# Eleven scan slots in place of fourteen for every 64 projection steps

## The chip, the cores and the metric

The kernel runs on one NeuronCore of a Trainium2 chip. TensorE (PE) multiplies matrices and writes to PSUM; PEld is its loading of the stationary operand; VectorE (DVE), ScalarE (ACT) and GpSimd (POOL) do the elementwise work; SyncE (SP) issues the DMAs. The metric is the device time of one execution in microseconds, the median of several runs.

## The reference

A trunk of two layers works on 256 tokens of width 2048. Each layer normalizes x, projects it to one wide row, passes that to two groups of heads and projects their joined output back onto x:

```python
for l in range(DEPTH):
    h = rms_norm(x, norm_g[l])
    proj = jnp.einsum('btd,dc->btc', h, w_in[l])
    rw_in, g_rw, q, k_at, v_at, g_at = jnp.split(proj, col_splits, axis=-1)
    ...
    y_rw = rwkv7_branch(r, k, v, xw, xa, ...)
    ...
    y_at = window_attention(qh, kh, vh, sink[l]).astype(x.dtype)
    mix = jnp.concatenate([y_rw * jax.nn.silu(g_rw), y_at * jax.nn.silu(g_at)], axis=-1)
    x = x + jnp.einsum('btc,cd->btd', mix, w_out[l])
return rms_norm(x, final_g)
```

The first group has 16 heads of 64 with a recurrent state, once forwards and once backwards in time:

```python
def step(S, inp):
    r_t, w_t, k_t, v_t, kk_t, a_t = inp
    s_kk = jnp.einsum('bhvk,bhk->bhv', S, kk_t)
    S = (S * w_t[:, :, None, :]
         - s_kk[..., None] * (a_t * kk_t)[:, :, None, :]
         + v_t[..., None] * k_t[:, :, None, :])
    return S, jnp.einsum('bhvk,bhk->bhv', S, r_t)
```

The sum of both directions is normalized per head; a bonus term times v is added. The second group is attention in a band of 128 tokens with a sink logit per head.

## The kernel before

**Projections.** The activations lie transposed, 16 tiles of 128 channels by 256 tokens. The kernel wants more than one rounded product gives, so every operand is split into a high part and a remainder (XH, XL and MH, ML for the activations; hi, lo for the weights), and one step is three products of 128x128 by 256 columns (L292 to L294, in `gemm`). An output tile of 128 columns takes 16 steps. `wsplit` makes the weights' parts, hi on ScalarE (L222) and lo on VectorE (L224), one half tile (8 steps) at a time, with two buffers. `Stream.run(n)` emits the next n steps; `Stream.later(n, f)` calls f after n steps.

**Scan.** The recurrence is computed in four chunks of 64 tokens (NC) for a pair of heads at a time; NP = 8 pairs in a layer, with both directions in one tile. It has three generators, and every `yield` in them is a place where the projections may go on:
- `scan_p(p)` prepares: low-rank products (pza, L671 to L673), decays (VectorE's scans), head sums (pk), scaled keys (BK, MV), the bonus (pbn). 13 parts.
- `scan_i(p)` forms the Gram rows GE of the chunks (pg, L786, masked by L792), transposes (pt: L809 the centred values, L817 the keys), and inverts a unit triangular matrix over six levels. The levels swap between products of TC into QF (L899, with a turn L866) and products of QF back into TC (L908, taken in by VectorE's L910); at the end come pf, then pn and its copy VF. 16 parts.
- `scan_b(p)` carries the state SUV through the four chunks: L957, copied to RH; L964, L970, L973, copied into SUV by L975; L980, taken by VectorE into the next chunk's state (L982); and the output products L987 into py. Then the norm of py: squares with row sums (L998), a power on GpSimd (L1000), the multiply by it, the products L1007, and the last steps into MH and ML. 17 parts.

**The order of work.** TensorE's order is the program's order, written out by hand: `manual_schedule` covers PE. For the other engines a planner orders the instructions by its own costs and by priority; `high_priority` lifts single ones, and what is called through PA or PV keeps the program's order among itself. Each engine then runs its list in order. `window(64, ...)` (L394) spreads the parts of several generators over SLOTS = 14 slots; after each slot's parts it runs 64/14 (4 or 5) projection steps. `scans(w)` says which pairs are in which phase in window w: preparation of pair w-1 (its tail, pair w-2), `scan_i` of pair w-2 in all slots and its last two parts at the start of the next window, `scan_b` of pair w-3 from slot 1 on, and its last four parts one window on. The order of the list of stages is the order of emission within a slot. Window 12 has attention alone; windows 10 and 11 have it beside the scan's end. After window 12 the output projection runs by itself (256 steps). ROT spreads the set-up of the rotary tables over layer 0's windows.

**Memory.** Tiles of a tag with `bufs=n` rotate over n buffers; a write waits until the readers of the tile n takings ago are done. `big` has four operand tiles of 16 by 256 floats a partition: X0, then XH, XL, MH, ML of the layers in turn. In PSUM, `ps_main` holds two projection tiles, `ps_w` two pairs of banks that all of `scan_p`, `scan_i` and the attention take in turn (`wpair`, `wbank`), and `ps_c` one bank for the state (pcc) and one for the output sums (py).

Of the kernel before, what the change touches and what calls it, by code (L numbers as in the profile page):

```python
# [21 lines left out]
T = 256  # L22
# [33 lines left out]
ROT = {0: [2, 3], 1: [], 7: [3, 6, 9], 8: [1, 4], 9: []}  # L56
# [78 lines left out]
def hybrid_trunk_kernel(ctx, tc, xT, wi, wv, wo, par, fing, dup, iup, sink, pos, cst, out):  # L135
# [11 lines left out]
    big = pool("big", 4)  # L147
# [31 lines left out]
    def bigt(dt, name):  # L179
        return big.tile([128, NKT, T], dt, tag="big", name=name)  # L180
# [123 lines left out]
    X0 = bigt(F32, "X0")  # L304
# [13 lines left out]
    AB, AL, QF = (cp.tile([128, 2, NC, 64], F16, name=n) for n in ("AB", "AL", "QF"))  # L318
# [289 lines left out]
    def queue_output(l):  # L608
# [4 lines left out]
        def tile_of(k):  # L613
# [6 lines left out]
            def evac(pm):  # L620
                if last and k == 0:
                    L.X2 = bigt(F32, "X2")
# [3 lines left out]
                if k == 0:  # L626
                    to.norm = Norm()
                    to.acc = st("acc", [T])
                    if not last:
                        to.XH, to.XL = bigt(F32R, "XH"), bigt(F32R, "XL")  # L630
# [24 lines left out]
    def layer(l):  # L655
# [3 lines left out]
        L.MH, L.ML = MH, ML = bigt(F32R, "MH"), bigt(F32R, "ML")  # L659
# [30 lines left out]
        def scan_p(p, t):  # L690
# [9 lines left out]
            LW = st("lw", [2 * T])  # L700
# [32 lines left out]
            BK = st("bk", [2, NC, 3, 64])  # L733
            km = st("lw", [2 * T])
# [14 lines left out]
            PA.activation(BK8[64:128, :, 0, :], BK8[64:128, :, 2, :], AF.Copy)  # L749
            yield  # L750
# [13 lines left out]
            bonus = high(km[:, 0:T], "th")  # L764
# [11 lines left out]
        def scan_i(p, t):  # L776
            VV, BK, MV = t["v"], t["BK"], t["MV"]
            flat = lambda x: x.rearrange("p d c j -> p (d c) j")
            GE = st("ge", [2, 2, NC, 2, 64], bufs=2)
# [26 lines left out]
            for b in range(2):  # L806
                for q in range(2):
                    for h in range(2):
                        PE.matmul(  # L809
                            pts[h][half[q], 384 + b * 64 : 448 + b * 64], VV[half[h], cs(2 * b + q)], cen[half[h], half[h]], start=True, stop=True  # L810
                        )

# [10 lines left out]
            SUV = st("suv", [2, NC, 2, 64], bufs=2)  # L823
            t["SUV"] = SUV
            for h in range(2):
                for q in range(2):
                    A.activation(
# [418 lines left out]
```

## Time and profile before

| what | us |
|---|---|
| median of 3 runs (lowest, highest) | 1187.84 (1186.2, 1188.79) |
| span of the profiled execution | 1186.6 |
| PE, DVE, ACT busy in it | 1160.9, 908.2, 777.3 |
| a scan window in steady state (one pair in each phase) | 41.2 |
| output projection of the last layer, to its last product | 90.5 |

The profile gives single times of one execution, the median is over others. Rows that begin with a time are instructions in order of time: start, duration, engine, line, operation, result and operands, tile shape on the array, size, count in a row, and in brackets idle time and what ended it. Matmuls overlap, so a row's duration is not its cost; the distance from start to start is. Rows that begin with a line number are groups of like instructions: total busy time, mean ns of one, and idle time before them by what ended it.

### The profile page before, as it was taken

What the parts mean: (1) busy time and instruction counts of PE and PEld (TensorE: products, weight loads), DVE (VectorE), ACT (ScalarE), POOL (GpSimd) and SP (SyncE); (2) the same over time, 40 slices, a digit from 0 to 9 for tenths busy, and PEclk for the clock granted to TensorE, in tenths of its full rate; (3) what the DMA queues carried; (4) which work ended last, traced back from release to release, by engine and by line L of the source; (5) the groups of instructions that cost most, each with busy time, mean ns of one, the idle gap of its engine ahead of it and who ended that gap; (6) DMA issues with size and microseconds to landing.
All of it is one profiled execution on the core that took longest, in us unless ns stands there. A gap on an engine that the chain in (4) does not pass through costs nothing.

```text
span 1186.6 us, 38095 instructions
## 1 busy us (share of the span) xinstructions
PE 1160.9 (98%) x16151; PEld 1082.7 (91%) x16151; DVE 908.2 (77%) x2017; ACT 777.3 (66%) x1955; POOL 18.7 (2%) x23
## 2 busy tenths in 40 slices
PE   8999999999999999999999999999999999999996
PEld 6988998999889989899999999999999998889996
DVE  6889878987877678766677988887887866786654
ACT  6666776777776666645555766876777666665553
POOL 0000000000000000000000000000000000000000
PEclk9999999999999999999999999999999999999998
DMA  7553333333323434477664443333323334345653
GB/s 257 164 170 123 109 107 116 108 98 115 109 94 122 136 117 142 134 234 236 210 184 165 134 131 114 95 113 117 122 83 109 122 124 132 114 145 190 213 185 123
DMA packets 60410, 166.63 MB, mean 140 GB/s; under 512 B 7728, under 2 KB 22736, under 8 KB 60240
## 3 DMA queue, kind: packets, MB, share of 16 engines
q1 hardware_dynamic: 60240, 164.21, 43.0%
q8 instruction: 126, 2.06, 0.7%
q14 instruction: 44, 0.36, 0.1%
HBM read 157.37 MB, written 4.19 MB: 136 GB/s over the span
## 4 chain that ended last, share of the span: by engine, by line
PE 74%; issue 15%; DVE 7%; ACT 2%; POOL 1%; DMA 1%; SPq 0%; DVEq 0%; POOLq 0%; ACTq 0%
PE pm L292 19%; PE pm L294 16%; PE pm L293 16%; PE pg L786 3%; DVE lo L224 2%; PE pcc L957 2%; PE py L987 2%; PE py L964 1%; PE pcc L980 1%; PE pq L899 1%; PE pcc L970 1%; PE pd L908 1%; PE pza L671 1%; POOL yv L1000 1%; PE pscr L1050 1%
## 5 line engine op out<-in xcount | busy, mean ns | idle before, releaser
L292 PE MATMUL pm<-XH,hi 128*128 128x256 f32 x1664 | 494.2, 297 | 3.9 <-ACT XH L184 1.6
L294 PE MATMUL pm<-XH,lo 128*128 128x256 f32 x1664 | 467.8, 281 | 5.9 <-DVE lo L224 5.8
L293 PE MATMUL pm<-XL,hi 128*128 128x256 f32 x1664 | 467.6, 281 | 0.8 <-DVE XL L185 0.6
L222 ACT ACTIVATE hi<-raw 128x512 fp32r<-128x512 f32 x560 | 328.2, 625 | 190.6 <-PE pm L293 91.8
L224 DVE TENSOR_TENSOR lo<-raw,hi 128x512 fp32r<-128x512 f32 x560 | 369.1, 686 | 102.5 <-ACT hi L222 95.2
L292 PEld LDWEIGHTS pm<-XH,hi 128*128 128x128 f32 x1664 | 313.4, 188 | 19.3 <-ACT XH L184 2.6
L294 PEld LDWEIGHTS pm<-XH,lo 128*128 128x128 f32 x1664 | 313.9, 189 | 8.3 <-DVE lo L224 8.3
L293 PEld LDWEIGHTS pm<-XL,hi 128*128 128x128 f32 x1664 | 314.1, 189 | 1.7 <-DVE XL L185 1.7
L292 PE MATMUL pm<-MH,hi 128*128 128x256 f32 x512 | 144.0, 281 | 0.0
L294 PE MATMUL pm<-MH,lo 128*128 128x256 f32 x512 | 143.8, 281 | 0.0
L293 PE MATMUL pm<-ML,hi 128*128 128x256 f32 x512 | 143.8, 281 | 0.0
L292 PEld LDWEIGHTS pm<-MH,hi 128*128 128x128 f32 x512 | 96.6, 189 | 0.8 <-issue 0.8
L293 PEld LDWEIGHTS pm<-ML,hi 128*128 128x128 f32 x512 | 96.6, 189 | 0.0
L294 PEld LDWEIGHTS pm<-MH,lo 128*128 128x128 f32 x512 | 96.6, 189 | 0.0
L910 DVE CAST_PREDICATED tv<-LV,pd 128x256 f16<-128x256 uint8 x80 | 34.2, 428 | 12.0 <-PE pd L908 11.4
L1065 ACT ACTIVATE mv<-mv,mx 128x257 f32<-128x257 f32 x64 | 31.9, 503 | 17.2 <-DVE mx L1062 17.2
L792 DVE TENSOR_TENSOR ge<-pg,C 128x1024 f32<-128x1024 f32 x32 | 38.8, 1219 | 2.3 <-PE pg L786 2.3
L975 ACT ACTIVATE suv<-pcc 64x128 f32<-64x128 f32 x128 | 34.3, 268 | 9.2 <-PE pcc L973 7.4
L959 ACT ACTIVATE rh<-pcc 128x128 f32<-128x128 f32 x64 | 17.5, 274 | 34.0 <-PE pcc L957 33.6
L902 ACT ACTIVATE QF<-pq 128x256 f16<-128x256 f32 x80 | 30.8, 384 | 12.5 <-PE pq L866 11.7
L786 PE MATMUL pg<-mv,bk 64*128 64x128 f32 x512 | 37.2, 285 | 0.3 <-DVE ge L792 0.3
L786 PEld LDWEIGHTS pg<-mv,bk 64*128 64x128 f32 x512 | 31.1, 187 | 2.4 <-DVE ge L792 0.4
(248 smaller groups left out, 1856.5 us busy)
## 6 DMA issues: line engine op xcount, KB each, us to landing
raw<-wi SPq DMA_DIRECT2D x207, 512.0 KB, 3.7
raw<-wo SPq DMA_DIRECT2D x64, 512.0 KB, 4.2
raw<-wv SPq DMA_DIRECT2D x8, 512.0 KB, 3.6
rrot<-u SPq DMA_DIRECT2D x80, 32.0 KB, 1.9
vg<-xT SPq DMA_DIRECT2D x16, 128.0 KB, 4.1
xd<-vg SPq DMA_DIRECT2D x16, 128.0 KB, 3.5
vg<-xd SPq DMA_DIRECT2D x16, 128.0 KB, 3.6
g<-dup SPq DMA_DIRECT2D x16, 97.0 KB
```

Of the source, the lines that this page charges most:

```text
L222: A.activation(hi[:, q], raw[:, q], AF.Copy)
L224: V.tensor_tensor(lo[:, q], raw[:, q], hi[:, q].bitcast(F32), op=ALU.subtract)
L292: PE.matmul(pm, wh, rh[:, kk, :], start=(kk == 0), stop=False)
L293: PE.matmul(pm, wh, rl[:, kk, :], start=False, stop=False)
L294: PE.matmul(pm, wl, rh[:, kk, :], start=False, stop=(kk == 15))
L786: PE.matmul(pg[:, h, c * 128 : (c + 1) * 128], BK[half[h], d, c, 1 - h : 3 - h, :].rearrange("p s j -> p (s j)"), MV[half[h], d, c].rearra ...
L792: V.tensor_tensor(GEd(d), pg.rearrange("p h (c x) -> p h c x", c=NC), gm[d].unsqueeze(1).unsqueeze(1).to_broadcast([128, 2, NC, 128]), op= ...
L902: A.activation(t_sub(QF), flat4(pq[:, :, 0:128]), AF.Copy)
L910: V.copy_predicated(t_sub(TC), t_mask, flat4(pd[:, :, 0:128]))
L957: PE.matmul(pc[half[h], 0, d, :], GE[h][r, d, ci[d], 0, :], SUV[r, d, ci[d], h, :], start=True, stop=True)
L975: A.activation(here(h), pc[half[h], 1], AF.Copy)
L1065: A.activation(Sc[:, h, q, 0:257], Sc[:, h, q, 0:257], AF.Exp, scale=0.125, bias=mx[:, q : q + 1], accum_out=den[:, q : q + 1])
```

## The change

The scan gets 11 slots in a window; each is followed by 5 or 6 projection steps. The preparation's last five parts move to the following window; `scan_i` has its last five parts in the following window's slots 0 to 4, and `scan_b` runs from slot 5 of that window through slot 10 of the next, so three pairs are in flight. The rows GE, the states SUV and the inversion's TC, TT and AB get another buffer each. The operand tiles are split in halves of 8; the preparation's scratch (LW, km, BK) lies in the half that X0 and later ML leave free (s0b), and every third pair's GE in the half that MH needs only for attention (s1b). The centred values (L809 and its four copies into SUV) move from `scan_i` to `scan_p`. The output products of chunk i are issued with the next chunk's first products. Attention's third score tile takes a GE buffer.

```diff
-SLOTS = 14
-
-STAGE_P = (([6], [4, 5, 6, 7, 8, 9, 10, 11, 12, 13]), ([2], [2]))
-STAGE_P0 = (([], [12, 13]), ([3], [3, 5, 6, 8, 10, 11, 12, 13]))
-STAGE_I = (list(range(SLOTS)), [0, 1])
-STAGE_B = (list(range(1, 14)), [1, 2, 3, 4])
+SLOTS = 11
+
+STAGE_P = (([7], [5, 6, 7, 8, 8, 9, 10]), ([6], [0, 1, 3, 6]))
+STAGE_P0 = (([], [9, 10]), ([2], [2, 4, 5, 7, 9]))
+STAGE_I = (list(range(SLOTS)), [0, 1, 2, 3, 4])
+STAGE_B = (list(range(5, SLOTS)), list(range(SLOTS)))
 ATT = [
-    [4, 11],
-    [1, 3, 6, 8, 11, 13],
-    [0, 2, 5, 7, 8, 10, 12, 13],
+    [3, 9],
+    [1, 3, 5, 6, 8, 10],
+    [0, 2, 4, 5, 6, 8, 9, 10],
 ]
-ROT = {0: [2, 3], 1: [], 7: [3, 6, 9], 8: [1, 4], 9: []}
+ROT = {0: [2, 3], 1: [], 7: [2, 5, 7], 8: [1, 3], 9: []}
...
-    big = pool("big", 4)
+    big = pool("big", 1)
...
+    def hold(tag, dt, name, shape=(NKT // 2, T)):
+        return big.tile([128, *shape], dt, tag=tag, name=name)
+    class Rows:
+        def __init__(self, tag, dt, name, parts=2):
+            self.tag, self.dt, self.name, self.t = tag, dt, name, []
+            for _ in range(parts):
+                self.more()
+        def more(self):
+            i = "ab"[len(self.t)]
+            self.t.append(hold(self.tag + i, self.dt, self.name + i))
...
-        L.MH, L.ML = MH, ML = bigt(F32R, "MH"), bigt(F32R, "ML")
+        L.MH, L.ML = MH, ML = Rows("s1", F32R, "MH", 1), Rows("s0", F32R, "ML", 1)
+        FR = hold("s0b", F32, "FR", (8 * T,))
...
-            LW = st("lw", [2 * T])
+            LW = FR[:, 0 : 2 * T]
...
-            BK = st("bk", [2, NC, 3, 64])
-            km = st("lw", [2 * T])
+            BK = FR[:, 2 * T : 8 * T].rearrange("p (d c s j) -> p d c s j", d=2, c=NC, s=3)
+            km = FR[:, 0 : 2 * T]
...
+            SUV = st("suv", [2, NC, 2, 64], bufs=3)
+            t["SUV"] = SUV
+            vt = wpair("vt")
+            for b in range(2):
+                for q in range(2):
+                    for h in range(2):
+                        PE.matmul(vt[half[q], h, b * 64 : b * 64 + 64], VV[half[h], cs(2 * b + q)], cen[half[h], half[h]], start=True, stop=True)
...
-            bonus = high(km[:, 0:T], "th")
+            bonus = high(km[:, 0:T], "pp")
...
-            GE = st("ge", [2, 2, NC, 2, 64], bufs=2)
+            AB = (AB0, AB1)[p % 2]
+            if p % 3 == 2:
+                GE = hold("s1b", F32, "GE", (2, 2, NC, 2, 64))
+            else:
+                GE = st("ge", [2, 2, NC, 2, 64], bufs=2)
...
-            TC = st("tv", [2, NC, 64], F16)
-            TT = st("tt", [2, NC, 64], F16)
+            TC = st("tv", [2, NC, 64], F16, bufs=2)
+            TT = st("tt", [2, NC, 64], F16, bufs=2)
...
+            def outputs(i):
+                for d in range(2):
+                    for h in range(2):
+                        c = order[d][i]
+                        PE.matmul(
+                            py[half[h], c, :], GE[h][:, d, c, 1, :], SUV[:, d, c, h, :],
+                            start=(i == 0 and d == 0), stop=(i >= NC // 2), skip_group_check=True,
+                        )
...
                 A.activation(RH, pc[:, 0], AF.Copy)
+                if i == 1:
+                    pyt = ps_c.tile([128, 512], F32, tag="y", name="py")
+                    py = pyt[:, 0:256].rearrange("p (c j) -> p c j", j=64)
+                if i > 0:
+                    outputs(i - 1)
                 yield
...
-                for d in range(2):
-                    for h in range(2):
-                        PE.matmul(
-                            py[half[h], ci[d], :], GE[h][:, d, ci[d], 1, :], SUV[:, d, ci[d], h, :],
-                            start=(i == 0 and d == 0), stop=(i >= NC // 2), skip_group_check=True,
-                        )
-                if i < NC - 1:
                     yield
+            outputs(NC - 1)
...
-            stages += [(4, scan_b, STAGE_B[1]), (3, scan_i, STAGE_I[1]), (3, scan_b, STAGE_B[0])]
-            stages += [(2, scan_i, STAGE_I[0])]
+            stages += [(4, scan_b, STAGE_B[1]), (3, scan_i, STAGE_I[1]), (2, scan_i, STAGE_I[0])]
+            stages += [(3, scan_b, STAGE_B[0])]
...
-            Sc = t["S"] = st("mv", [2, 2, 264], bufs=3)
+            Sc = t["S"] = st("ge", [2, 2, 264], bufs=2) if j == 2 else st("mv", [2, 2, 264], bufs=3)
...
+            for x in (MH, ML):
+                x.more()
...
-            window(64, *scans(w), *([(setup_, ROT.get(w, [3, 6, 12, 12]))] if l == 0 else []))
+            window(64, *scans(w), *([(setup_, ROT.get(w, [2, 5, 9, 9]))] if l == 0 else []))
```

More of the change, by code (lines that the diff above doesn't have):

```diff
@@ L177, in hybrid_trunk_kernel, with __getitem__ @@
     gm = (cc("gmf"), cc("gmb"))
-    def bigt(dt, name):
-        return big.tile([128, NKT, T], dt, tag="big", name=name)
+    def hold(tag, dt, name, shape=(NKT // 2, T)):
[8 more added lines that the diff above has]
+            self.t.append(hold(self.tag + i, self.dt, self.name + i))
+        def __getitem__(self, at):
+            p, k, t = at
+            n = NKT // 2
+            if isinstance(k, slice):
+                return self.t[k.start // n][p, k.start % n : (k.stop - 1) % n + 1, t]
+            return self.t[k // n][p, k % n, t]
     def x_split(XH, XL, x, k, l):
@@ L317, in hybrid_trunk_kernel @@
     LV = cp.tile([128, NL, 2, 128], U8, name="LV")
[L318 removed]
+    AB0, AB1, AL, QF = (cp.tile([128, 2, NC, 64], F16, name=n) for n in ("AB0", "AB1", "AL", "QF"))
     MSK = cp.tile([128, NC, 64], F16, name="MSK")
```

32 lines of the change are left out of this document (11 added, 21 removed).

## The prediction, made before the changed kernel was run

> **What bounds the kernel.** I read the page first, then the views by stage, then TensorE in order of time.
>
> ```profile
> span 1186.6 us, 38095 instructions
> PE 1160.9 (98%) x16151; PEld 1082.7 (91%) x16151; DVE 908.2 (77%) x2017; ACT 777.3 (66%) x1955; POOL 18.7 (2%) x23
> PE 74%; issue 15%; DVE 7%; ACT 2%; POOL 1%; DMA 1%; SPq 0%; DVEq 0%; POOLq 0%; ACTq 0%
> 632.20:658.30 26.10, 24.80 (x213) 23.95 (x211) 23.03 (x45) 15.28 (x32) 0.00 (x0) 1.00 0.50 170
> 816.30:857.50 41.20, 41.17 (x753) 37.87 (x751) 34.03 (x72) 29.92 (x81) 1.01 (x1) 1.00 0.34 110
> 1082.50:1173.00 90.50, 90.50 (x765) 90.50 (x764) 52.00 (x94) 47.72 (x93) 0.00 (x0) 1.00 0.59 187
> ```
>
> The last three rows are stages of layer 1: scan window 1, scan window 6, the output projection (columns: stretch, length, busy us of PE, PEld, DVE, ACT, POOL, granted clock, DMA share, GB/s). TensorE is the bound in all. In the output stage nothing but projection products run: 90.5 us for 765 is 0.118 us each. Window 6 holds 192 such, 22.7 us; the other 18.5 us are the scan's small products. The clock is 1.00, so all that can be won is in the number and cost of those 18.5 us, and in waits. VectorE has 34.0 of 41.2 us.
>
> Next, what an interruption of the projection costs. A "run" is the small products between two projection products. I take the start of the last projection product ahead of it to the start of the second one behind it, less two pitches (0.24). First the six-level inversion's product alone (L908), then a scan product alone (L957), then both in one run:
>
> ```profile
> 812.06 0.28 PE L294 MATMUL pm<-XH,lo 128*128 128x256 f32 x1
> 812.28 0.30 PE L908 MATMUL pd<-QF,tt 64*64 64x32 f16 x16
> ...
> 812.73 0.28 PE L293 MATMUL pm<-XL,hi 128*128 128x256 f32 x1
> 995.78 0.28 PE L294 MATMUL pm<-XH,lo 128*128 128x256 f32 x1
> 995.99 0.45 PE L957 MATMUL pcc<-suv,ge 128*64 128x64 f32 x8
> ...
> 996.59 0.28 PE L293 MATMUL pm<-XL,hi 128*128 128x256 f32 x1
> 796.33 0.28 PE L294 MATMUL pm<-XH,lo 128*128 128x256 f32 x1
> ...
> 797.38 0.28 PE L293 MATMUL pm<-XL,hi 128*128 128x256 f32 x1
> ```
>
> L908 alone: 0.67 - 0.24 = 0.43 us. L957 alone: 0.81 - 0.24 = 0.57. Together: 1.05 - 0.24 = 0.81. One joined run instead of two saves **0.19 us**. These two use the array in different tile shapes (64*64 and 128*64). Two groups of one shape save more:
>
> ```profile
> 997.76 0.28 PE L294 MATMUL pm<-XH,lo 128*128 128x256 f32 x1
> 997.97 0.45 PE L964 MATMUL py<-suv,mv 64*64 64x64 f32 x8
> ...
> 999.03 0.28 PE L293 MATMUL pm<-XL,hi 128*128 128x256 f32 x1
> 790.25 0.28 PE L294 MATMUL pm<-XH,lo 128*128 128x256 f32 x1
> 790.46 0.45 PE L964 MATMUL py<-suv,mv 64*64 64x64 f32 x8
> ...
> 791.63 0.28 PE L293 MATMUL pm<-XL,hi 128*128 128x256 f32 x1
> ```
>
> The group L964/L970/L973 alone takes 1.27 - 0.24 = 1.03; with L908 in its run 1.38 - 0.24 = 1.14. L908 adds 0.11, not 0.43: a joint of one shape saves **0.32 us**.
>
> Last, the waits that TensorE does have in the windows:
>
> ```profile
> 804.26 0.45 PE L957 MATMUL pcc<-suv,ge 128*64 128x64 f32 x8
> 804.64 0.30 PE L899 MATMUL pq<-tv,AB 64*64 64x32 f16 x16
> ...
> 809.31 0.69 PE L987 MATMUL py<-suv,ge 128*64 128x64 f32 x8
> 809.94 0.30 PE L899 MATMUL pq<-tv,AB 64*64 64x32 f16 x16
> 812.57 0.42 DVE L237 TENSOR_TENSOR ysq<-py,yv 128x256 f32<-128x256 f32 x1 [1.19 <-POOL yv L1000]
> 814.12 0.42 DVE L910 CAST_PREDICATED tv<-LV,pd 128x256 f16<-128x256 uint8 x1
> 814.26 0.28 PE L294 MATMUL pm<-XH,lo 128*128 128x256 f32 x1
> 814.59 0.30 PE L866 MATMUL pf<-EYE,tv 64*64 64x32 f16 x16
> 434.08 0.42 DVE L237 TENSOR_TENSOR ysq<-py,yv 128x256 f32<-128x256 f32 x1 [1.19 <-POOL yv L1000]
> 436.61 0.40 PE L294 MATMUL pm<-XH,lo 128*128 128x256 f32 x1 [1.01 <-DVE lo L224]
> L866 PEld LDWEIGHTS <-tv 64*64 64x64 f16 x1280 | 17.8, 109 | 4.6 <-DVE tv L910 3.6
> ```
>
> Small, and three kinds. The last output product (L987 of chunk 3) takes 0.63 from its start to L899, where L957 of the same shape and count took 0.38: 0.25 us of waiting for the state that ScalarE has just copied. The turn at the end of the inversion starts 0.33 after the product ahead of it, not 0.22: 0.11, for L910, which stood behind VectorE's 1.19 us of waiting for GpSimd's power (the last row, a group over the whole span, has 3.6 us of such waits before all turns). And at the start of window 11 the same 1.19 us makes a weight remainder late: about 1.1 us.
>
> **The change, part by part.**
>
> *Fewer, fuller runs.* In a steady window one pair in each phase passes 33 groups of small products (the projections' lookalikes pza, pk and pbn left out: full array, they save nothing by joining). They stand in 14 runs now, so 19 joints; in 11 slots, 22 joints. Written out by slot, the new joints are: between groups of one shape 12 (now 9), of different shapes 10 (now 10). So three joints of one shape more per window, 3 x 0.32 = 0.96 us; at the other price 3 x 0.19 = 0.57. Per layer, windows 2 to 9 lose three runs each (24), window 10 two, window 1 gains one (the centred values now stand alone there), and window 11 gains five, because the last pair's state scan now reaches through all its slots: 24 + 2 - 1 - 5 = 20. For two layers 40 x 0.32 = **12.8 us** off; lower bound 40 x 0.19 = 7.6. I take the upper, since every joint that is new in the list is of one shape.
>
> *Longer slots.* A slot goes from 41.2/14 = 2.94 to about 40.1/11 = 3.65 us; each chain step has 0.7 us more to come back. The three waits above are all shorter than that. L987: 0.25 in nine windows, 2.3 us. The turn: of the 3.6 us I count two thirds, 2.4. Window 11: 1.1 twice, 2.3; there the power's reader also moves away from the attention's sums. Together **7.0 us** off, at least 3 if VectorE's order keeps some. In window 1 VectorE has 23.0 of 26.1 us; the bonus sums, three passes like ysq's 0.42 or 1.3 us, go to the next window: 0.5 off, between 0 and 2.6.
>
> *Output products a slot later.* As many products, next to L957 instead of L980; both joints are 128*64, so no cost. Their bank is then taken in slot 8, one slot behind the norm's last reader in slot 7: hidden by a 3.65 us slot; without that cover some 0.6 us a window, one ScalarE pass like lw's 0.60 below.
>
> *Centred values moved into the preparation.* 16 products and four copies (0.38 each, below) move from slot 2 to slot 9, and take a PSUM pair of their own: 20 takings of the two pairs in a window, not 19. Two slots pass before that pair is needed again: nothing; if the copies came late, up to 1.5 us.
>
> *Third buffers, the scratch in the free operand half, the bonus in another tag.* No instruction added; they let three pairs be in flight. Buffers still single (AL, QF, VF, the state's bank) are each written a slot or more after their last reader in the new order, or later in the same TensorE order. The gate tile is let go in slot 8, not 2, and taken again at the window's end: two slots. No DMA is added, removed or moved past another on SP's queue, and the rotary set-up keeps its number of steps. A window asks for the same bytes in 1.1 us less, 110 to 113 GB/s, under the 187 of the output stage: nothing.
>
> *What the squeeze costs.* Five preparation steps stand in slots 7 to 10 with two in slot 8, and the first Gram product follows in slot 0, where three slots lay between. Rows for both engines:
>
> ```profile
> 806.45 0.68 DVE L237 TENSOR_TENSOR mv<-kr,pp 128x512 f32<-128x512 f32 x1
> 789.15 0.60 ACT L237 ACTIVATE lw<-pza 128x512 f32<-128x512 f32 x1 [0.85 <-PE pza L673]
> 789.64 0.83 ACT L237 ACTIVATE th<-pza,DP 128x256 f32<-128x256 f32 x2
> L222 ACT ACTIVATE hi<-raw 128x512 fp32r<-128x512 f32 x560 | 328.2, 625 | 190.6 <-PE pm L293 91.8 <-issue 68.6 <-PE pm L294 9.2
> L827 ACT ACTIVATE suv<-pt 64x256 f32<-64x256 f32 x64 | 24.3, 379 | 0.7
> L792 DVE TENSOR_TENSOR ge<-pg,C 128x1024 f32<-128x1024 f32 x32 | 38.8, 1219 | 2.3 <-PE pg L786 2.3
> ```
>
> The last preparation product (mv) ended 2.9 us after its slot opened (804.26 to 807.13). In the new order the Gram product comes 3.65 + 0.8 = 4.4 us after: it fits, with 1.5 to spare. Tighter is the pair of pza, the last group of slot 5. Slot 6 takes that pair again, 5 projection steps (1.8) and pbn (0.3) later, about 2.2 us with the edges. ScalarE needs 1.3 us (789.15 to 790.47), and one 0.63 weight pass ahead makes 1.95; with two, 2.6, a wait of 0.4. TensorE's order is fixed, so everything behind L899 waits too. New waits then lie between 0 and 0.63 us in each of 18 windows, 0 to 11 us. I take 0.25 a window, **4.5 us** on, the size of the wait at L987 now.
>
> Sum: -12.8 - 7.0 - 0.5 + 4.5 = -15.8 us. On the profiled execution's span: 1186.6 - 15.8 = 1170.8. The median of the runs, 1187.84, lies 1.2 above that span, so **1172 us**.
>
> **Rivals.**
>
> 1. *Only the joints pay.* The waits change place instead of going, and joints save 0.19: -7.6, **1180 us**. For it: VectorE is 83% busy in a window, and lumps of work stay lumps. Against it: the L987 wait is on ScalarE's copy alone and has 0.7 us more.
>
> 2. *The squeeze takes it all back.* New waits of about 1.1 us in each of the 18 windows (2 to 10 of each layer), 20 us: **1187.5 us**, no change. This is also the case in which three pairs are in flight by name only, because a single buffer or a PSUM pair ties them together. Against it: by rows, the takings are two per slot at most, as in slots 0 to 2 now, where 0.1 us is lost.
>
> 3. *The emptying of PSUM becomes the bound: slower.* Place: slots 5 and 6, the pza pair, in every window. If the four norm sums of the older pair (now in the same slot) and two weight passes go ahead of pza's three passes on ScalarE, the pair comes free 1.7 + 1.25 + 1.3 = 4.2 us after pza where 2.2 are there; some of the norm sums run beside pza's own 1.4 us, so about 1.5 us of wait. 18 x 1.5 = 27 against 20.3 of gain: **1194 us**. It decides the sign from 1.13 us a window (20.3/18). The 1.7 us are these:
>
> ```profile
> 810.10 0.22 ACT L998 ACTIVATE ysq<-py 128x64 f32<-128x64 f32 x1 [0.59 <-PE py L987]
> 810.82 0.22 ACT L998 ACTIVATION_READ_ACCUMULATOR ysq<-py 128x1 f32 x1
> ```
>
> (first and last of eight, here 0.94 us from end to end; 1.7 is the eight durations added up, the unfavourable bound.) The Trainium skill, page "TensorEngine Tiling (Array Packing)", section "PSUM Bottleneck", says that packing small products speeds TensorE but not the emptying of PSUM, whose copies may become the bottleneck. By that rule the time would be that of this rival; the trace of before agrees only in part, with waits of 0.1 to 0.25 us a window beside 18.5 us of small products.
>
> **How the numbers follow.** The forecast gets 0.56, rival 1 0.21, rival 2 0.09, rival 3 0.14. This kernel's measurement can tell about 0.2% (2.4 us) from no change. Faster: 0.56 + 0.21 = 0.77; same 0.09; slower 0.14. The range: low, 12.8 + 7.0 + 2.6 off and no new wait, 1187.8 - 22.4 = 1165; high, rival 1 with 5 us of new waits, 1185. It leaves out rival 3 and most of rival 2.
>
> **What would show it.** Steady windows of 40 to 40.3 us, not 41.2, and 11 runs in each; L987 of chunk 3 back at 0.38; the turn 0.22 behind its projection product; window 11 without its 1 us stop. The number of runs is certain, their price is the first thing to check: window time less 22.7 should be 17.2 to 17.6. The forecast is wrong if TensorE shows waits at L899 in slot 6 for ScalarE, at L786 in slot 0 for VectorE, or at L294 for a late remainder, adding up to more than 0.5 us a window; or if joints in the new neighbourhoods cost what separate runs do.

## The result, and the profile after

| | before | after |
|---|---|---|
| median of 4 runs (lowest, highest), us | 1187.62 (1186.2, 1188.79) | 1197.62 (1197.45, 1197.86) |
| span of the profiled execution, us | 1186.6 | 1196.1 |
| a steady window of layer 1, us | 41.2 | 41.8 |
| steady windows of layer 0 (numbers 4 to 7), us | 41.4 to 41.6 | 42.2 to 43.0, and one of 47.2 |

The ratio is 1.0085, with an interval of 1.0071 to 1.0099: slower by 10 us, where 16 us of gain were forecast. A window runs here from its first projection product to that of the next, found by the count of steps in the trace. Times are medians; of the runs below, one execution of 2709 us, against 1255 to 1259 us in the same kernel's three others, is left out as slow. The kernel before has medians of 1187.0 to 1188.1 us in the sets of executions below, so a comparison with the kernel after is good to about 1 us. Most line numbers of the kernel after are 20 to 38 higher: gemm's three products are L312 to L314, the weight remainder lo L244, the first Gram product pg L824, the inversion's product pd L931 and its copies L893 and L925, the output products, which were L987, are now L972.

The page of the kernel after:

```profile
span 1196.1 us, 38078 instructions
PE 1156.7 (97%) x16151; PEld 1079.4 (90%) x16151; DVE 910.7 (76%) x2017; ACT 773.9 (65%) x1955; POOL 18.5 (2%) x23
PE 59%; DVE 17%; issue 15%; ACT 5%; DMA 3%; SPq 0%; POOL 0%; DVEq 0%; POOLq 0%; ACTq 0%
```

The same instructions, nearly the same busy times. What changed is the last row, the chain that ended last: VectorE had 7% of it, now 17%, ScalarE 2%, now 5%. TensorE's share fell. Somebody now waits for VectorE who did not. The stages of layer 1 in the kernel after (window 1, window 5, output projection; columns as in the prediction):

```profile
642.10:667.30 25.20, 25.03 (x228) 24.26 (x227) 22.41 (x43) 16.75 (x37) 0.00 (x0) 1.00 0.53 172
782.34:824.13 41.79, 40.69 (x752) 37.44 (x750) 34.25 (x72) 29.70 (x81) 1.01 (x1) 1.00 0.33 108
1093.00:1183.00 90.00, 90.00 (x769) 90.00 (x768) 52.00 (x94) 47.73 (x93) 0.00 (x0) 1.00 0.59 188
```

The output stage is what it was. In the steady window TensorE is busy for 40.69 of 41.79 us, where before it was 41.17 of 41.20. So the runs did get cheaper, and idle time came in. Who is waited for stands in the view of waits of the kernel after (us in total, times, longest):

```profile
PE pg L824 <- DVE mv L257: 11.6, 11, 1.8
PE pm L314 <- DVE lo L244: 6.6, 15, 1.1
PEld pm L314 <- DVE lo L244: 12.9, 28, 1.3
PE pd L931 <- ACT tt L893: 1.9, 1, 1.9
```

The first row is new: the same Gram product waited 0.3 us in all before. Rows of PE and of PEld tell partly of the same stop, so they are not added. In layer 1 I took the waits of a steady window from the starts of TensorE's products instead: 0.76 us at pg in slot 0, and at late remainders 0.65 and then 0.14 in slot 7 and 0.24 in slot 9. Together that is 1.75 to 1.8 us; I count **1.75 us a window** (after each late remainder the next product comes another 0.1 late, which is counted in).

The three old waits went as forecast. The last output products and the inversion's product behind them, in the kernel after:

```profile
799.30 0.45 PE L972 MATMUL py<-suv,ge 128*64 128x64 f32 x8
799.69 0.30 PE L931 MATMUL pd<-QF,tt 64*64 64x32 f16 x16
```

0.39 us from start to start, where L987 took 0.63. In the groups the turn's idle time fell from 4.6 to 1.2 us (the second row; the first is the Gram product's weight load, whose idle time was 2.4):

```profile
L824 PEld LDWEIGHTS pg<-mv,FR 64*128 64x128 f32 x512 | 31.1, 187 | 13.6 <-DVE mv L257 10.0 <-issue 1.8 <-PE pd L931 0.9
L889 PEld LDWEIGHTS <-tv 64*64 64x64 f16 x1280 | 17.9, 110 | 1.2
```

Why VectorE is late is seen in the steady window cut into eleven equal pieces of 3.8 us (5 to 10 of 0 to 10 here; a piece lies some 2 us behind the slot of its number, for the parts of slot 5 begin with the L972 above at 799.30). After the length, the third number of a row is VectorE, the fourth ScalarE:

```profile
801.30:805.10 3.80, 3.80 (x67) 3.59 (x67) 1.41 (x4) 3.17 (x9) 0.85 (x1) 1.00 0.34 126
805.10:808.90 3.80, 3.54 (x59) 3.09 (x58) 3.77 (x9) 3.74 (x11) 0.00 (x0) 1.00 0.03 6
808.90:812.70 3.80, 3.67 (x67) 3.37 (x68) 3.73 (x7) 3.11 (x10) 0.00 (x0) 1.00 0.26 85
812.70:816.50 3.80, 3.80 (x75) 3.60 (x74) 3.80 (x10) 2.70 (x8) 0.00 (x0) 1.00 0.48 156
816.50:820.30 3.80, 3.80 (x65) 3.40 (x64) 3.79 (x10) 3.73 (x12) 0.00 (x0) 1.00 0.34 116
820.30:824.10 3.80, 3.09 (x58) 2.70 (x57) 3.74 (x8) 2.36 (x7) 0.00 (x0) 1.00 0.36 99
```

VectorE is 82% busy over the window, and the prediction had its load only in this form, as 83%. But it has 1.41 of 3.8 us in piece 5, and then 18.83 of 19.0 us in the five pieces behind it. A list that is full can't make up for a late start. Chosen single instructions of the same window, VectorE's and ScalarE's among TensorE's (others between them are left out):

```profile
803.00 0.42 DVE L454 TENSOR_TENSOR u<-pm,rb 128x256 f32<-128x256 f32 x1 [2.00 <-PE pm L314]
...
807.47 1.14 ACT L242 ACTIVATE hi<-raw 128x512 fp32r<-128x512 f32 x2
808.30 0.68 DVE L244 TENSOR_TENSOR lo<-raw,hi 128x512 fp32r<-128x512 f32 x1
809.03 0.39 PE L314 MATMUL pm<-XHb,lo 128*128 128x256 f32 x1 [0.40 <-DVE lo L244]
...
818.33 0.30 PE L922 MATMUL pq<-tv,AB 64*64 64x32 f16 x16
...
822.30 0.68 DVE L257 TENSOR_TENSOR mv<-kr,pp 128x512 f32<-128x512 f32 x1
823.04 1.16 PE L824 MATMUL pg<-mv,FR 64*128 64x128 f32 x16 [0.71 <-DVE mv L257]
```

First VectorE stands idle for 2.00 us, because the next item of its list is the evacuation of a projection tile that isn't ready. After one more stop of 0.66 it runs without a gap from 804.08 on. The weight remainder (808.30) follows a high part that ScalarE made late, and L314 waits. Of the two passes at 807.47 the first ends at about 808.1, and VectorE was at the remainders of the low-rank inputs until 808.30: so its own list holds this remainder for about 0.2 us of the stop, and ScalarE's list for the rest. At the end mv, the preparation's last product, ends at 822.98, 4.65 us after slot 10 opened with L922 (818.33); pg was due at about 822.3, 4.0 after it, and waits 0.71. Before, the full stretch was as full, but shorter (from piece 6 to 10, five of 2.94 us), and two pieces with room followed it. The kernel before, window 6, pieces 10 to 12 of 0 to 13:

```profile
845.73:848.67 2.94, 2.94 (x76) 2.71 (x74) 2.92 (x6) 1.76 (x6) 0.00 (x0) 1.00 0.03 6
848.67:851.62 2.95, 2.95 (x75) 2.65 (x68) 2.29 (x6) 2.33 (x11) 0.00 (x0) 1.00 0.53 178
851.62:854.56 2.94, 2.94 (x38) 2.78 (x39) 1.75 (x5) 2.48 (x11) 1.01 (x1) 1.00 0.47 156
```

### The profile page after: what moved, and what is told of

It reads as the page before. It is cut to its first block, busy times and chain, and to the rows that moved or that the text cites. A ratio compares the mean times of both kernels' runs of the same rounds, so it can differ in the third digit from the quotient of the medians.

```text
span 1196.1 us, 38078 instructions
## 1 busy us (share of the span) xinstructions
PE 1156.7 (97%) x16151; PEld 1079.4 (90%) x16151; DVE 910.7 (76%) x2017; ACT 773.9 (65%) x1955; POOL 18.5 (2%) x23
## 3 DMA queue, kind: packets, MB, share of 16 engines
q8 instruction: 126, 2.06, 0.7%
## 4 chain that ended last, share of the span: by engine, by line
PE 59%; DVE 17%; issue 15%; ACT 5%; DMA 3%; SPq 0%; POOL 0%; DVEq 0%; POOLq 0%; ACTq 0%
PE pm L312 14%; PE pm L314 13%; PE pm L313 12%; DVE lo L244 5%; PE pg L824 3%; DVE FR L257 2%; DVE kd L257 2%; DMA raw<-wi 1%; DVE mv L257 1%; PE pcc L987 1%; PE py L999 1%; PE py L972 1%; PE pza L692 1%; DVE suv L1017 1%; PE pscr L1078 1%
## 5 line engine op out<-in xcount | busy, mean ns | idle before, releaser
L244 DVE TENSOR_TENSOR lo<-raw,hi 128x512 fp32r<-128x512 f32 x560 | 369.3, 686 | 110.5 <-ACT hi L242 104.9
L312 PE MATMUL pm<-XHa,hi 128*128 128x256 f32 x832 | 247.0, 297 | 2.8 <-ACT XHa L204 2.0
L312 PE MATMUL pm<-XHb,hi 128*128 128x256 f32 x832 | 244.6, 294 | 2.6 <-ACT hi L242 2.6
L314 PE MATMUL pm<-XHb,lo 128*128 128x256 f32 x832 | 238.5, 287 | 7.0 <-DVE lo L244 6.6
L313 PE MATMUL pm<-XLb,hi 128*128 128x256 f32 x832 | 234.6, 282 | 0.0
L313 PE MATMUL pm<-XLa,hi 128*128 128x256 f32 x832 | 234.2, 282 | 0.3 <-DVE XLa L205 0.3
L314 PE MATMUL pm<-XHa,lo 128*128 128x256 f32 x832 | 233.8, 281 | 0.1
L312 PEld LDWEIGHTS pm<-XHa,hi 128*128 128x128 f32 x832 | 157.2, 189 | 14.4 <-ACT XHa L204 3.4
L314 PEld LDWEIGHTS pm<-XHb,lo 128*128 128x128 f32 x832 | 158.1, 190 | 13.0 <-DVE lo L244 12.2
L312 PEld LDWEIGHTS pm<-XHb,hi 128*128 128x128 f32 x832 | 158.1, 190 | 8.7 <-ACT hi L242 3.2
L313 PEld LDWEIGHTS pm<-XLb,hi 128*128 128x128 f32 x832 | 158.2, 190 | 0.3 <-DVE XLb L205 0.3
L313 PEld LDWEIGHTS pm<-XLa,hi 128*128 128x128 f32 x832 | 157.3, 189 | 1.0 <-DVE XLa L205 1.0
L314 PEld LDWEIGHTS pm<-XHa,lo 128*128 128x128 f32 x832 | 157.1, 189 | 0.4 <-DVE lo L244 0.4
L314 PE MATMUL pm<-MHa,lo 128*128 128x256 f32 x256 | 71.8, 280 | 0.1
L312 PE MATMUL pm<-MHa,hi 128*128 128x256 f32 x256 | 71.9, 281 | 0.0
L312 PE MATMUL pm<-MHb,hi 128*128 128x256 f32 x256 | 71.6, 280 | 0.0
L314 PE MATMUL pm<-MHb,lo 128*128 128x256 f32 x256 | 71.6, 280 | 0.0
```

The costliest lines, as they stand in the source:

```text
L244: V.tensor_tensor(lo[:, q], raw[:, q], hi[:, q].bitcast(F32), op=ALU.subtract)
L312: PE.matmul(pm, wh, rh[:, kk, :], start=(kk == 0), stop=False)
L313: PE.matmul(pm, wh, rl[:, kk, :], start=False, stop=False)
L314: PE.matmul(pm, wl, rh[:, kk, :], start=False, stop=(kk == 15))
```

## Layer 0's window 7

The 47.2 us have a second cause. In that window the rotary set-up needs a sine and a cosine, and ScalarE changes its function table for them and back. The kernel after, chosen rows of ScalarE and TensorE in order of time:

```profile
303.88 1.28 ACT L257 ACT_TABLE_LOAD   x1
305.18 0.42 ACT L257 ACTIVATE SIN<-SIN 128x256 f32<-128x256 f32 x1
...
308.30 0.38 ACT L893 ACTIVATE tt<-pq 128x256 f16<-128x256 f32 x1
308.73 0.30 PE L931 MATMUL pd<-QF,tt 64*64 64x32 f16 x16 [1.90 <-ACT tt L893]
...
310.34 1.28 ACT L257 ACT_TABLE_LOAD   x1
```

With the new list the first load comes at 303.88, behind the evacuation of pza and at the end of piece 5; in the steady window above ScalarE is busy for 3.17 of 3.8 us in that piece and for 3.74 in the next. The inversion's copy (308.30) comes late and L931 stops for 1.90 us. Then the clock fell, as the stretches of the same window show (the granted clock is the number after the five busy times):

```profile
304.00:308.00 4.00, 2.83 (x35) 2.56 (x34) 2.82 (x7) 3.91 (x9) 0.00 (x0) 1.00 0.00 0
308.00:312.00 4.00, 2.15 (x30) 1.78 (x31) 2.94 (x8) 3.97 (x8) 0.00 (x0) 0.80 0.00 0
312.00:316.00 4.00, 4.00 (x60) 3.74 (x60) 4.00 (x7) 2.20 (x5) 0.00 (x0) 0.50 0.39 135
316.00:320.00 4.00, 4.00 (x72) 3.75 (x72) 2.02 (x6) 2.60 (x7) 0.00 (x0) 0.84 0.41 131
```

TensorE is busy for 2.83 and 2.15 of 4 us, and late in the second stretch the clock falls: the means are 0.80, 0.50 and 0.84, and from 310.44 to 317.26 it is 0.50. Against full speed these three rows lose 4 x (0.20 + 0.50 + 0.16) = 3.4 us of clock, part of it while TensorE stood still anyway: an estimate of 3 us.

## The experiments

All edits are against the kernel after. Theory A: the preparation, pressed into slots 6 to 10, makes VectorE late for pg and for the remainders. Theory B: the new buffers and PSUM takings, or the moved outputs, cost something of themselves. Theory C: layer 0's excess is the place of the rotary set-up.

### Fourteen slots with everything else new

```diff
-SLOTS = 11
+SLOTS = 14
...
```

The lists STAGE_P, STAGE_P0, STAGE_I, STAGE_B, ATT and ROT and the order of the stages are put back too.

> The changed kernel's buffers, scratch, centred values in the preparation and output products a slot later, but with the slot lists and the stage order of before (14 slots). Theory A: what cost time is the new order of slots, so this is near the kernel before, 1184 to 1192 us, with windows of 41 to 41.6. Theory B: it is slow too, above 1194.

1187.95 us, ratio 1.000 (0.9991 to 1.001). A steady window of layer 1:

```profile
776.59:817.54 40.95, 40.95 (x752) 37.66 (x751) 34.13 (x72) 29.82 (x81) 1.01 (x1) 1.00 0.34 111
```

TensorE has no gap, and the window is 0.25 us shorter than before: the output products a slot later pay by themselves what the prediction gave for the wait at L987. It comes to nothing over the whole program, because windows 1 and 2 of layer 1 are longer by 0.6 and 0.75 us and the steady windows of layer 0 are as long as before (41.4 to 41.65 us). Theory B is out in this form: all 10 us of loss come from what was put back, the lists of slots and the order of stages. The run doesn't test the new buffers with three pairs in flight, but in the kernel after no wait of a steady window is at a buffer or a PSUM pair.

### The rotary set-up moved

Alone in window 7, and then in all windows of layer 0, into slots where VectorE and ScalarE have room:

```diff
-ROT = {0: [2, 3], 1: [], 7: [2, 5, 7], 8: [1, 3], 9: []}
+ROT = {0: [2, 3], 1: [], 7: [1, 2, 7], 8: [1, 3], 9: []}
```

> The changed kernel with the sine and cosine of the rotary tables in slot 2 of window 7 of layer 0, not slot 5. Theory C (their two table loads of 1.28 us fall between pza's evacuation and the inversion's copies, TensorE stops for 2.6 us and its clock drops): window 7 of layer 0 goes from 47.2 to about 42.9 us, total about 1193. Rival: the stop comes from the clump in slots 5 to 7 alone, and window 7 stays above 46.

1191.65 us (1.0035, 1.0022 to 1.0048): 6.0 us less than the kernel after. Window 7 falls from 47.2 to 42.4 us.

```diff
-ROT = {0: [2, 3], 1: [], 7: [2, 5, 7], 8: [1, 3], 9: []}
+ROT = {0: [2, 3], 1: [], 7: [1, 2, 4], 8: [1, 3], 9: []}
...
-ROT.get(w, [2, 5, 9, 9])
+ROT.get(w, [0, 3, 4, 5])
```

> The changed kernel with the rotary set-up of layer 0 in slots 0, 3, 4 and 5 of windows 2 to 6 (where VectorE has idle time), not 2, 5, 9 and 9, and the sine in slot 2 of window 7. If VectorE's clump is what layer 0 pays more for, its windows 4 to 6 fall from 42.2 to 43 us to those of layer 1, 41.8, and the total to about 1188. If the set-up costs its passes wherever it stands, they stay near 43 and the total is that of the sine alone, 1191.7.

1188.44 us (1.0003, 0.9993 to 1.0012): 9.2 us less. Layer 0's window 5 is now:

```profile
191.91:233.76 41.85, 40.71 (x753) 37.43 (x751) 35.16 (x76) 29.77 (x81) 1.01 (x1) 1.00 0.33 108
```

That is layer 1's 41.8. So theory C holds: 9.2 of the lost 10 us came from where the set-up was put, 6.0 of them from the place of the sine and cosine in window 7. What is left is a kernel equal to the one before, not 16 us faster.

### VectorE's load taken away

The reciprocal in the preparation, 1.76 us of VectorE in slot 7, is left out; one pass of 0.42, which writes a constant, stands in its place:

```diff
-            PV.reciprocal(KD, pk[:, 0:T])
+            PV.tensor_scalar(KD, pk[:, 0:T], 0.0, 1e-4, op0=ALU.mult, op1=ALU.add)
```

> The changed kernel with the reciprocal of the key norms (VectorE, 1.76 us a pair) left out: a constant stands in its place, by one pass of about 0.4 us. Theory A (VectorE has more work in slots 6 to 10 than fits): the wait of the first Gram product in slot 0 (0.76 us) goes and the late remainder of slot 9 with it, the one in slot 7 (0.65 us) stays, since it comes before; windows of layer 1 at 40.8 to 41.0 us, not 41.8, total 1181 to 1185. Rival (the order of VectorE's list and not its load): less than 0.3 us a window.

1182.6 us (0.9954, 0.9939 to 0.9969), 15.0 less than the kernel after. The waits of this kernel:

```profile
PE pm L314 <- DVE lo L244: 6.7, 15, 1.2
PE pg L824 <- DVE mv L257: 1.4, 3, 0.6
```

pg's wait is down from 11.6 us to 1.4; the steady window of layer 1 is 40.7 us. The stops in slots 0 and 9 are gone, the first one in slot 7 (0.55 + 0.1) has stayed. Without that too it would be 40.7 - 0.65 = 40.05, the window that the prediction named. So 1.3 us of VectorE's load in the full stretch decide about 1.1 us of each window.

### Moving the load within the list

Of the eight parts of the preparation that stand in slots 5 to 10, three of the last four a slot earlier, so that slot 7 has three parts and slot 8 two:

```diff
-STAGE_P = (([7], [5, 6, 7, 8, 8, 9, 10]), ([6], [0, 1, 3, 6]))
+STAGE_P = (([7], [5, 6, 7, 7, 8, 8, 9]), ([6], [0, 1, 3, 6]))
```

> Only the last four of the eight parts earlier (parts 5 to 8 in slots 7, 8, 8, 9); pza and the head sums stay. Theory A: the wait of the first Gram product in slot 0 goes, the late remainder in slot 7 stays or grows; windows of layer 1 at about 41.0 us, total about 1190. If the remainder in slot 7 is ScalarE's lateness (the weight parts hi stand behind the norm sums and pza's passes), it is unchanged here at 0.65 us. Theory B: no change.

1209.15 us (1.0179, 1.0164 to 1.0194): a miss. Its waits:

```profile
PE pm L314 <- DVE lo L244: 23.3, 29, 1.8
```

pg's wait is gone, and in its place the stop at the remainder of slot 9 is 1.44 us, where it was about 0.2; steady windows of layer 1 take 42.6. Moving work inside a full list moved the wait from one reader to another, and made it longer. In layer 0 they take 44.5, and part of that is the clock, as window 5 of both layers shows (0.96 and 1.00):

```profile
199.12:243.59 44.47, 42.31 (x752) 38.77 (x750) 35.28 (x76) 29.78 (x80) 1.01 (x1) 0.96 0.32 101
792.30:834.90 42.60, 40.85 (x752) 37.39 (x750) 34.35 (x72) 29.67 (x80) 1.01 (x1) 1.00 0.34 108
```

The whole preparation a slot earlier, so that it begins in VectorE's idle slot:

```diff
-STAGE_P = (([7], [5, 6, 7, 8, 8, 9, 10]), ([6], [0, 1, 3, 6]))
+STAGE_P = (([6], [4, 5, 6, 7, 7, 8, 9]), ([6], [0, 1, 3, 6]))
```

> All eight early preparation parts one slot earlier (slots 4 to 9, not 5 to 10), so that they use the time in which VectorE now stands idle in slots 4 and 5. Theory A (VectorE's preparation work is clumped into slots 6 to 10 and is late): the waits of the first Gram product (0.76 us) and of the weight remainder in slot 7 (0.65 us) go, steady windows of layer 1 fall from 41.8 to about 40.4 us, total about 1181 us. Theory B (three pairs in flight, the buffers and the planner's order cost it, wherever the preparation stands): windows stay at 41.8 and the total within 3 us of 1197.6.

1255.31 us (1.0575, 1.0557 to 1.0592), the worst of all, for a reason that I had not seen. Timeline, waits and window 5 of layer 1 of this kernel:

```profile
847.65 0.41 DVE L257 TENSOR_TENSOR bv<-pbn,vg 128x256 f32<-128x256 f32 x1
...
848.12 0.30 PE L922 MATMUL pq<-tv,AB 64*64 64x32 f16 x16 [3.71 <-DVE bv L257]
```

```profile
PE pq L922 <- DVE bv L257: 50.5, 14, 4.9
PE pza L692 <- ACT vf L960: 10.0, 12, 0.9
```

```profile
821.62:867.93 46.31, 41.68 (x752) 38.68 (x750) 34.51 (x73) 30.11 (x80) 1.05 (x1) 0.96 0.30 97
```

pk, pbn and pq now fall into one slot and take three pairs of PSUM banks where the ring has two. pq needs the pair that pbn holds until VectorE has read it, and TensorE stands for 3.71 us. In slot 4 pza comes third behind pn and pq, and waits up to 0.9 us for the copy of pn. The steady window takes 46.3, and an estimated 1.8 us of that is the clock (0.96 over the window, so 0.04 of 46.3). Over the whole span the mean granted clock is 0.968, where the kernel before has 0.995: by an estimate 0.027 x 1253.5 = 34 of the 67 us of loss. pg and the remainders don't wait in this window, but VectorE had the time of TensorE's stops to catch up; the experiment therefore decides nothing on theory A. It says why the preparation can't simply start sooner: slots 0 to 4 already have two takings each.

Last, the high parts of the weights first on ScalarE, to remove the stop in slot 7, on top of the rotary set-up in idle slots:

```diff
-            A.activation(hi[:, q], raw[:, q], AF.Copy)
             with tc.high_priority(offset=PRIO_LO):
+                A.activation(hi[:, q], raw[:, q], AF.Copy)
```

> Eleven slots with the rotary set-up in the idle slots and with the weights' high parts (ScalarE) at the priority that their remainders (VectorE) have, so that ahead of slot 7 they come before the inversion's copies and the V tile's low-rank parts. If the late remainder in slot 7 is ScalarE's list (the high part stands behind it), that wait of 0.65 us goes, windows of layer 1 fall from 41.8 to 41.1 us and the total from 1188 to about 1178. If VectorE's full list is the cause, the wait stays or moves and the windows are 41.6 or more.

1190.91 us (1.0035, 1.0016 to 1.0054). Waits:

```profile
PE pm L314 <- DVE lo L244: 8.9, 16, 0.9
PE pd L931 <- ACT tt L893: 6.4, 12, 1.0
```

The stop in slot 7 went to the product next to it: L931 now waits 0.54 for the copy that the weight part pushed back, and a remainder in slot 9 waits 1.0. The windows grow to 42.2. ScalarE's piece 6 is as full as VectorE's (3.74 and 3.77 of 3.8 us in the kernel after).

### Twelve and thirteen slots

Is there a number of slots between that pays? Each with lists of its own:

```diff
-SLOTS = 11
+SLOTS = 12
...
+STAGE_P = (([6], [4, 5, 6, 7, 8, 9, 10, 11]), ([5], [0, 2, 5]))
+STAGE_I = (list(range(SLOTS)), [0, 1, 2, 3])
+STAGE_B = (list(range(4, SLOTS)), list(range(9)))
```

> The changed kernel's buffers with 12 slots: the first preparation part in slot 4, one part per slot to slot 11, three in the next window, so that the same VectorE work spreads over eight slots of 3.4 us, not five of 3.8; takings of the PSUM pairs never three in a slot; sine in slot 2. Theory A: windows of layer 1 at 40.4 to 40.8 us (two runs fewer than 14 save 0.5, and no wait over 0.3), total 1175 to 1182. Rival (three pairs in flight do not fit into fewer than 14 slots): windows of 41.2 or more, total not under 1187.

1195.17 us (1.0061, 1.0045 to 1.0078), a miss. Steady windows take 41.3 us and hold one wait:

```profile
804.23 0.30 PE L931 MATMUL pd<-QF,tt 64*64 64x32 f16 x16 [0.77 <-ACT tt L893]
```

The inversion's copies stand behind the key rows' copies on ScalarE. Without that wait the window would be 40.5. The steady windows are as long as before, so the loss lies elsewhere, most of all in window 10: 39.2 and 37.8 us in the two layers, 35.4 and 35.5 before.

```diff
-SLOTS = 11
+SLOTS = 13
...
+STAGE_P = (([6], [4, 5, 6, 7, 8, 9, 10, 11, 12]), ([3], [1, 3]))
+STAGE_I = (list(range(SLOTS)), [0, 1, 2])
+STAGE_B = (list(range(3, SLOTS)), list(range(7)))
```

> The same with 13 slots, preparation over slots 4 to 12. Theory A: windows of layer 1 at 40.6 to 40.9 us, total 1179 to 1184. Rival: as 14 slots, 1187 to 1188.

1193.46 us (1.0049, 1.0034 to 1.0064), a miss too: 41.8 us a window, with stops of 0.75 for the same copy and 0.26 in slot 2. Then the twelve slots with those copies lifted, and the first attention scores of window 10 two slots earlier:

```diff
-                A.activation(t_sub(QF), flat4(pq[:, :, 0:128]), AF.Copy)
-                if turned:
-                    turned()
+                with tc.high_priority(offset=PRIO_TC):
+                    A.activation(t_sub(QF), flat4(pq[:, :, 0:128]), AF.Copy)
+                    if turned:
+                        turned()
```

> The twelve-slot kernel with a higher priority for ScalarE's copies of the inversion (QF and the turn), which stood behind two copies of key rows in slots 6 and 7, and with the first attention scores in slot 1 of window 10. If that list is what TensorE waits for in slot 7 (0.84 us a window), windows of layer 1 fall from 41.3 to 40.5 us, the stop of 1.95 us in window 10 goes, total 1178 to 1184. If the wait comes from the load and only moves, windows stay at 41.0 or more, total above 1188.

1191.82 us (1.0032, 1.0023 to 1.0041). The wait at L931 is gone, a remainder near the window's end waits 0.74 + 0.1 in its place, and the steady window is 41.3 as it was.

### Two products on GpSimd

GpSimd is idle, and two products of the preparation read no PSUM. They go there, on top of the rotary set-up in idle slots; in a second kernel the remainders of the low-rank inputs too:

```diff
-            PV.tensor_tensor(dd(km), dd(km), two(K), op=ALU.mult)
+            G.tensor_tensor(dd(km), dd(km), two(K), op=ALU.mult)
...
-            PV.tensor_tensor(
+            G.tensor_tensor(
                 MV[:, :, :, 1, :], R.rearrange("p (c j) -> p c j", j=64).unsqueeze(1).to_broadcast([128, 2, NC, 64]), PP, op=ALU.mult
...
```

> The kernel with the rotary set-up in the idle slots, and two elementwise products of the preparation (keys times learning factor, 0.69 us, and receptances times decays, 0.68 us) issued on GpSimd, which is idle, not VectorE. Load theory: as without the reciprocal, 1.37 us leaves VectorE's full slots 6 to 10, the waits in slots 0 and 9 go and the one in slot 7 (0.55 + 0.1) stays: steady windows about 40.7 us in both layers, and 1188.4 - 16 x 1.1 = about 1171 us, which beats the kernel before. Rival, the two engines hinder each other or GpSimd is slow: VectorE's passes beside GpSimd's get longer by as much as was saved, or the first Gram product waits for GpSimd: windows stay at 41.8 or grow, 1188 us or more.

1202.37 us (1.0132, 1.0115 to 1.0149): the rival's case. GpSimd's and VectorE's rows in a steady window of this kernel:

```profile
808.06 1.29 POOL L785 TENSOR_TENSOR mv<-kr,pp 128x512 f32<-128x512 f32 x1 [7.57 <-ACT pp L257]
808.25 1.65 DVE L244 TENSOR_TENSOR lo<-raw,hi 128x512 fp32r<-128x512 f32 x1
813.04 1.60 POOL L768 TENSOR_TENSOR FR<-FR,kr 128x512 f32<-128x512 f32 x1 [3.68 <-issue]
813.42 1.50 DVE L257 SCALAR_TENSOR_TENSOR t<-t,vg 128x256 f32<-128x256 f32 x1
```

The two VectorE passes take 0.68 and 0.42 us in the kernel after. Here the second starts 0.38 after GpSimd's product and ends 0.28 after it (814.92 and 814.64): it stood still for about as long as GpSimd worked, and the first did the same. The two products took 1.37 us from VectorE's list, and the two passes got longer by 0.97 and 1.08. So the list is fuller than it was (VectorE's busy time in a steady window went from 34.2 to 35.1 us), just ahead of weight remainders: the first stop in slot 7, 0.65, stays, and the second one there and the one in slot 9 grow to 1.1 and 1.3. Steady windows take 43.1 us.

> The kernel before this one in the list, and the two remainders of the low-rank inputs (0.39 and 0.41 us on VectorE, just ahead of the late weight remainder of slot 7) on GpSimd too. Load theory: the weight remainder of slot 7 comes earlier by up to 0.55 us, windows of 40.2 to 40.7 us, 1164 to 1171 us. Rival, the remainder waits for ScalarE's high part and not for VectorE: slot 7 keeps its 0.55 and the time is that of the kernel with two products on GpSimd; if GpSimd's own passes are long, pza waits for them and it is slower.

1207.49 us (1.0172, 1.0153 to 1.019): slower again, though the steady windows are mostly 42.7. What is longer is windows 1 and 2 (in layer 1 26.7 and 38.1 us, 25.4 and 34.9 in the kernel of the two products), and the clock is 0.96 over that window 2. The stop in slot 7 remains (1.1 us), so this run doesn't tell apart whether VectorE or ScalarE holds that remainder: GpSimd's passes disturb VectorE in the same place. Only the rows at 807.47 and 808.30 above speak to it.

No version that computes the same result beat the kernel before; the one without the reciprocal is faster.

## Why the prediction was wrong

**Fewer, fuller runs (-12.8): right in the steady windows.** They have 11 runs. Priced run by run from the trace, a window's small products fell by 0.84 us, which is 0.28 a joint, where 0.32 was taken and 0.19 was the lower bound. Window time less the 22.7 us of projection products and less the 1.75 of waits is 17.3 us; 17.2 to 17.6 were named.

**Longer slots (-7.0): the waits went, one of them for another reason.** L987's wait is gone, also with fourteen slots, so it was the later place and not the longer slot; the turn's is down to a quarter, and window 11 has no stop of 1 us at its start.

**What the squeeze costs (+4.5): the step that failed, in size and place.** 0.25 us a window was taken, at the PSUM pair of pza in slot 6. Measured are 1.75, none of it at that pair: 0.76 at pg for VectorE's mv, the rest at remainders, and of these the first in slot 7 is held longer by ScalarE's list than by VectorE's. The step compared one number, mv's end 2.9 us after its slot opened, with the 4.4 us of room in the new order. But 2.9 belonged to the old list. In the new one it is 4.65, since the five steps ahead of it are packed into slots that VectorE's other work already fills; and the room came out as 4.0. The sum to make was that of VectorE's load by slot, with the moved passes in it: 18.83 of 19.0 us. At 40.05 + 1.75 the window is 41.8, as measured; removing 1.3 us of that load removed 1.1 us of waits. In windows 4 to 7 of both layers this is 8 x 1.5 = 12 us of the 25.8 between forecast and result (15.8 of gain forecast, 10.0 of loss measured).

**The rotary set-up (nothing): the second failure, 9.2 us.** Its steps were counted and found equal; where they fall was not looked at. The list by slot numbers put a table load of 1.28 us where ScalarE has little room, and VectorE's passes of the set-up into its full stretch: in layer 0's windows 4 and 6 pg waited 1.81 us, not the 0.7 to 0.8 of layer 1.

**The ends of a layer.** Windows 3 and 9 are shorter by 3.7 us in layer 1, windows 10 and 11 longer by 3.0. Window 11 was to grow by about 0.5 (five runs, less its stop) and grew by 2.5, in both layers, with three runs more, 7 to 10. The trace of layer 1 says why: work moved from the one to the other. The small products in window 11 rise from 120 to 188 and in window 10 from 220 to 320; in windows 3 and 2 they fall from 542 to 474 and from 370 to 270. Windows 3 and 11 together take 76.3 us, 76.4 before, so the growth of window 11 is no loss by itself. What the ends of a layer lose stands in windows 2 and 3 as waits of the same kinds, at pg, at remainders and at ScalarE's high parts: 2.1 and 0.8 us, where before had 0.5 and none. Less the 0.25 taken for each, that is about 1.9 us a layer. With 12 and 9.2, these 3.8 us make 25 of the 25.8; the tally is an estimate, in which the smaller differences of the other windows are taken to cancel.

**The rivals.** Rival 3 gave 1194 us, near the result, but for a wrong reason: ScalarE's emptying of pza stands in no row of waits of the steady windows. By the Trainium skill's rule ("TensorEngine Tiling (Array Packing)", "PSUM Bottleneck") the copies out of PSUM could have become the limit; this trace has VectorE's elementwise list as the limit for pg and for slot 9, most of which reads no PSUM. The rule agrees with other runs here: twelve and thirteen slots and the weight parts first, where L931 waits for ScalarE's copy out of PSUM (0.77 us with twelve), and the preparation a slot earlier, where L922 waits for VectorE to read pbn. Rival 2, no change, with waits of about 1.1 us in each of 18 windows, is near what remains once the rotary set-up is in order (1188.44 us, with 1.75 us of waits in each of the eight steady windows). The last sentence of the prediction named the rows that would refute it, and two of the three came, at L824 (then L786) and at L314 (then L294).

What stays open is whether an order of eleven slots exists that spreads VectorE's work well enough. By the window without waits, 40.05 us, it would be worth about 1.7 us in each steady window against the kernel after, 1.1 against the kernel before; none of the orders tried here reached it.

## What to carry to other kernels

Before a schedule with fewer and fuller slots is priced, add up the load of each in-order engine slot by slot with the moved work in it; a mean of 82% says little when five slots in a row are at 99% and their reader comes right behind them. In such a stretch a wait that was moved away came back at the next reader in the orders and priorities tried here; only less work there helped. Whatever is placed by slot number (table loads, set-up, PSUM takings) has to be placed anew when the slots change.

## What the runs showed of the hardware

TensorE's granted clock fell to half after short stops. In layer 0's window 7 TensorE was busy for 2.83 and 2.15 of 4 us, its longest idle time was 1.90 us, and the clock was 0.50 from 310.44 to 317.26; the estimate of what that cost is 3 us. In the last kernel, with the low-rank remainders on GpSimd too, it fell after a stretch of 3.41 us in which TensorE was busy for 2.06, with a longest stop of 1.35:

```profile
698.45:701.86 3.41, 2.06 (x45) 1.70 (x44) 3.41 (x8) 2.17 (x6) 0.00 (x0) 1.00 0.17 68
701.87:705.28 3.41, 3.41 (x18) 3.41 (x17) 1.85 (x4) 1.53 (x5) 0.00 (x0) 0.50 0.61 179
```

The Trainium skill ("TensorE: Matmul & The Clock Gate", "Part 1: The HAM clock gate") gives an idle window of about 3.4 us for this; in these two places no idle time was that long, and stops of 1.90 and 1.35 us, with the gaps around them, were enough.

VectorE and GpSimd hinder each other on operands in SBUF: 0.42 us became 1.50 beside a GpSimd product of 1.60, and 0.68 became 1.65 beside one of 1.29; each ended only after GpSimd's. The Trainium skill ("SBUF — State Buffer", "SBUF: two separate sides") calls the ports that the two share an exclusive lock, held for a whole instruction; these rows agree.

VectorE's reciprocal of 128x256 took 1.76 us, four times a product of that size (0.41).
